# The value matmuls of two attention pairs as one group in one PSUM bank, with the input that is made last read first

## The chip, the cores and the metric

The kernel runs on one core of one Trainium2 chip. The metric is the device time of an execution in microseconds (us); the time of a kernel is the median of its runs. Times inside an execution come from the trace of one profiled execution.

## The reference

One block of a streaming encoder, for 256 tokens of width 2048: a normalisation, one wide projection, then two branches side by side (an HGRN2 recurrence with 8 heads, and attention in chunks of 64 tokens with 16 heads), merged by gates, an output projection, and an MLP of width 8192. The change lies in the attention branch, between the projections of q, k and v (each 1024 wide) and the projection `w_branch_b`:

```
def chunk_band_attention(q, k, v, rel_bias):     # (B, H, T, Dh): H = 16, T = 256, Dh = 64
    # each chunk of 64 queries sees its own chunk and the 8 before it (all of the past, at T = 256)
    ...
    s = jnp.einsum('bhnqd,bhnkd->bhnqk', qc, kb).astype(jnp.float32) * (Dh ** -0.5) + bias[:, None]
    s = jnp.where(valid[:, None, :], s, -jnp.inf)
    p = jax.nn.softmax(s, axis=-1).astype(v.dtype)
    o = jnp.einsum('bhnqk,bhnkd->bhnqd', p, vb)
```

## The kernel before, in words

**The large projections.** Weights come from HBM in pieces `raw_...` by DMAs that SP issues. ACT casts each to fp32r (`wh_...`, L91) and DVE subtracts the cast from the original (`wl_...`, L92); this is `split`. PE then forms a product from a high and a low part: for q and k in `mm_t` (accumulators `acc_aq`, `acc_ak`; L178 with 512 columns for the high part, L183 with 256 for the low one), for the rest in `mm3` (L136 to L138, 512 columns each; `acc_av...` are the values v, `acc_ga0...` the first gate projection). These matmuls fill nearly all of PE's stream. `aq2` and `ak2` are the third quarter of q and k, and so on.

**Attention.** Sixteen heads go two at a time, as a pair; the pairs 0 to 3 are called 00 to 03, the pairs 4 to 7 10 to 13 (the first digit is the half of `yb` into which they go). `attn_pair` computes the scores of a pair (L595, eight short matmuls into PSUM tile `s00` ... `s13`) and calls `attn_head` twice. A head has 256 queries in two blocks of 128: the first sees 128 keys, the second 256, so its scores are 128 x 384. For each head:

- POOL fetches the bias (L601) and fills the corner with a large negative number (L602).
- DVE adds the bias (L604, L605) and takes the maxima (L607, L608).
- ACT takes exp with sums (L610, L611): 128 columns, then 256.
- DVE inverts the sums and scales the two blocks (L614, 128 columns, then L615, 256) in the SBUF tile `sb`, of which there are two.
- PE transposes the three blocks of 128 columns (L618) into a PSUM tile `tpp`; ACT copies it to SBUF (`pt`, L620; four buffers).

**The values.** `attn_values` multiplies the transposed probabilities of a pair with v, in a PSUM tile `pa`: four matmuls with 64 output rows each (L631). Two have 256 columns and take the keys 0 to 127 (`av00`, or `av10` for the second half), two have 128 columns and take the keys 128 to 255 (`av01`, `av11`); of each two the second head of the pair goes first. `split` then writes the result as high part (ACT cast) and low part (DVE subtraction) into `act_yb`, the left operand of the projection `w_branch_b`, which comes after the gate projections.

**What sets the order.** The tile framework schedules all instructions when the kernel is built, by priorities and its own estimates of time, so the order of each engine's queue is fixed, and every engine works its queue in that order. The scores and the values have a raised priority (`high_priority`). In the source, the values of a pair are called one pair later than its heads, and so stand behind the next pair's. `tpp` and `pa` share the two buffers of one PSUM pool (`ps_tp`, tag "tp"), so a new one of either kind needs the one before last to be read out.

Of the kernel before, what the change touches and what calls it, by code (L numbers as in the profile page):

```python
# [8 lines left out]
F32 = mybir.dt.float32  # L9
# [7 lines left out]
P = 128  # L17
T = 256
# [32 lines left out]
def tile_hybrid_block(  # L51
# [5 lines left out]
    nc = tc.nc  # L57
# [158 lines left out]
    for kt, n in zip(starts, steps):  # L216
        c, a = kt // 4, kt % 4
# [380 lines left out]
    def attn_head(hd, ps):  # L598
        bias = bp.tile([P, T], F32, name=f"bias{hd}", tag="bias", bufs=3)
        rb = rel_bias[hd]  # L600
        nc.gpsimd.dma_start(bias, bass.AP(tensor=rb.tensor, offset=rb.offset + P + 1, ap=[[1, P], [1, T]]))  # L601
        nc.gpsimd.memset(bias[0:CH, 0:CH], NEG)  # L602
        s = bp.tile([P, 3 * P], F32, name=f"sb{hd}", tag="s", bufs=2)
        nc.vector.tensor_tensor(s[:, 0:P], ps[:, 0:P], rev(bias[:, 0:P]), op=ALU.add)  # L604
        nc.vector.tensor_tensor(s[:, P:], ps[:, P:], rev(bias), op=ALU.add)  # L605
        mx = small.tile([P, 2], F32, name=f"mx{hd}", tag="mx")
        nc.vector.tensor_reduce(mx[:, 0:1], s[:, 0:P], axis=AX.X, op=ALU.max, negate=True)  # L607
        nc.vector.tensor_reduce(mx[:, 1:2], s[:, P:], axis=AX.X, op=ALU.max, negate=True)  # L608
        sums = small.tile([P, 2], F32, name=f"sum{hd}", tag="sums")
        nc.scalar.activation(s[:, 0:P], s[:, 0:P], AF.Exp, bias=mx[:, 0:1], accum_out=sums[:, 0:1])  # L610
        nc.scalar.activation(s[:, P:], s[:, P:], AF.Exp, bias=mx[:, 1:2], accum_out=sums[:, 1:2])  # L611
        rs = small.tile([P, 2], F32, name=f"rs{hd}", tag="rs")
        nc.vector.reciprocal(rs, sums)
        nc.vector.tensor_scalar(s[:, 0:P], s[:, 0:P], rs[:, 0:1], None, op0=ALU.mult)  # L614
        nc.vector.tensor_scalar(s[:, P:], s[:, P:], rs[:, 1:2], None, op0=ALU.mult)  # L615
        tp = ps_tp.tile([P, 3, P], F32, name=f"tpp{hd}", tag="tp")
        for i in range(3):
            nc.tensor.transpose(tp[:, i, :], s[:, i * P:(i + 1) * P], ident)  # L618
        pt = bp.tile([P, 3, P], F32, name=f"pt{hd}", tag="pt", bufs=4)
        nc.scalar.copy(pt, tp)  # L620
        return pt

    def attn_values(g, pr, pts, vs):

        hi, lo = yb[g][:, :, 0, :], yb[g][:, :, 1, :]
        po = ps_tp.tile([P, T], F32, name=f"pa{g}{pr}", tag="tp")
        with tc.high_priority(offset=2000):
            for i, src, dst in ((0, slice(0, 2), slice(0, T)), (1, slice(2, 3), slice(P, T))):
                for j, pt in ((1, pts[1]), (0, pts[0])):
                    r = slice(64 * j, 64 * j + 64)  # L630
                    nc.tensor.matmul(po[r, dst], vs[i][:, P * pr + 64 * j:P * pr + 64 * j + 64], pt[:, src, :].rearrange("p a t -> p (a t)"),  # L631
                                     start=i == 0, stop=i == 1, skip_group_check=True)
        split(hi[:, pr, :], lo[:, pr, :], po)

    def token(what, pool=None):
        if pool is not None:
# [77 lines left out]
    pairs = {}  # L714
# [229 lines left out]

    qT = [qk_chunk(C_AQ + i * T, f"aq{i}", rstd8_t, acc_q[i]) for i in range(2)]
    kT = [qk_chunk(C_AK + i * T, f"ak{i}", rstd_t) for i in range(2)]
    pts = None
    for i in range(4):
        if i > 1:
            qT.append(qk_chunk(C_AQ + i * T, f"aq{i}", rstd8_t))  # L950
# [2 lines left out]
            alone(Unit(lambda: xT, lambda: Sx, w_in_n, C_AV, "av", values))  # L953
        if not i % 2:
            yb.append(new_act(f"yb{i // 2}"))
        for pr in (2 * i, 2 * i + 1):
            last, pts = pts, attn_pair(pr // 4, pr % 4, qT[i][:, pr % 2, :], kT[i][:, pr % 2, :])
            if last:
                attn_values((pr - 1) // 4, (pr - 1) % 4, last, av[(pr - 1) // 4])
    attn_values(1, 3, pts, av[1])  # L960

    ga, gb = [], []
    units = []
# [247 lines left out]
```

## Time and profile before

| what | value |
|---|---|
| time, median of 3 runs | 1389.49 us (1389.38 to 1389.76) |
| profiled execution, own time | 1389.94 us |
| its span in the trace | 1388.1 us (1.84 us lie around it) |
| attention heads on PE, first transpose to last value group | 266.9 to 391.0 us |
| value matmuls (`pa`) | 64 records, first 304.9 us, last 390.7 us |
| casts of `pa` on ACT (L91) | 8, median 372 ns |
| subtractions of `pa` on DVE (L92) | 8, median 418 ns |
| transposes (`tpp`) | 48, median 273 ns |
| copies to `pt` on ACT (L620) | 16, median 479 ns |

How to read it: PE is busy nearly all the time, and the length that is shown for a matmul overlaps with the next one's (matmuls are pipelined). What a matmul costs PE's stream is therefore read from start to start, not from its length. A value matmul of the program leaves two records. The attention heads are spread thinly between the matmuls of the projections; in the trace's rows, `x8` counts the records that one row takes together.

### The profile page before, as it was taken

What the parts mean: (1) busy time and instruction counts of PE and PEld (TensorE: products, weight loads), DVE (VectorE), ACT (ScalarE), POOL (GpSimd) and SP (SyncE); (2) the same over time, 40 slices, a digit from 0 to 9 for tenths busy, and PEclk for the clock granted to TensorE, in tenths of its full rate; (3) what the DMA queues carried; (4) which work ended last, traced back from release to release, by engine and by line L of the source; (5) the groups of instructions that cost most, each with busy time, mean ns of one, the idle gap of its engine ahead of it and who ended that gap; (6) DMA issues with size and microseconds to landing.
All of it is one profiled execution on the core that took longest, in us unless ns stands there. A gap on an engine that the chain in (4) does not pass through costs nothing.

```text
span 1388.1 us, 18593 instructions
## 1 busy us (share of the span) xinstructions
PE 1376.7 (99%) x6550; PEld 1143.5 (82%) x6550; DVE 1137.7 (82%) x1417; ACT 922.7 (66%) x1185; POOL 143.4 (10%) x227
## 2 busy tenths in 40 slices
PE   9999999999999999999999999999999999999997
PEld 8889888878778888888888888888888888888886
DVE  7897988876878775698998977879877888878886
ACT  6765645665676664346777766678666876668864
POOL 3000001101100000001211011200011001110200
PEclk9999999999999999999999999999999999999999
DMA  9654446685669886558979789988899889998892
GB/s 328 235 178 141 163 166 239 169 284 169 175 199 284 261 266 226 189 168 273 301 215 310 245 259 300 261 255 244 251 298 295 248 223 263 276 297 265 255 276 105
DMA packets 124077, 331.61 MB, mean 239 GB/s; under 512 B 11072, under 2 KB 11840, under 8 KB 123600
## 3 DMA queue, kind: packets, MB, share of 16 engines
q1 hardware_dynamic: 103696, 265.59, 54.4%
q0 software_dynamic: 19568, 64.04, 23.5%
q8 instruction: 51, 0.84, 0.2%
q10 hardware_dynamic: 720, 0.81, 0.2%
q14 instruction: 42, 0.34, 0.1%
HBM read 271.67 MB, written 10.49 MB: 203 GB/s over the span
## 4 chain that ended last, share of the span: by engine, by line
PE 89%; DMA 5%; DVE 3%; issue 2%; ACT 1%; POOL 0%; POOLq 0%; SPq 0%; ACTq 0%; DVEq 0%
PE acc_ak L178 2%; PE acc_aq L178 2%; PE acc_hf L178 2%; PE acc_hq L178 2%; PE ps L415 1%; PE acc_ak L183 1%; PE acc_hg L137 1%; PE acc_hi L137 1%; PE acc_bb L136 1%; PE acc_hi L138 1%; PE acc_hg L136 1%; PE acc_bb L137 1%; PE acc_ba L136 1%; PE acc_hi L136 1%; PE acc_ba L138 1%
## 5 line engine op out<-in xcount | busy, mean ns | idle before, releaser
L178 PE MATMUL acc_aq<-act_x,wh_aq 128*128 128x512 f32 x128 | 41.7, 402 | 0.0
L178 PE MATMUL acc_hf<-act_x,wh_hf 128*128 128x512 f32 x128 | 40.8, 400 | 0.1
L178 PE MATMUL acc_hq<-act_x,wh_hq 128*128 128x512 f32 x128 | 40.7, 400 | 0.0
L178 PE MATMUL acc_ak<-act_x,wh_ak 128*128 128x512 f32 x128 | 40.4, 397 | 0.0
L91 ACT CAST wh_bb<-raw_bb 128x1024 fp32r<-128x1024 f32 x16 | 16.9, 1054 | 23.3 <-PE acc_ba L138 17.7
L92 DVE TENSOR_TENSOR wl_bb<-raw_bb,wh_bb 128x1024 fp32r<-128x1024 f32 x16 | 19.6, 1223 | 14.8 <-ACT wh_bb L91 14.8
L91 ACT CAST wh_ba<-raw_ba 128x1024 fp32r<-128x1024 f32 x16 | 16.8, 1052 | 19.9 <-PE acc_bb L138 13.8
L92 DVE TENSOR_TENSOR wl_aq<-raw_aq,wh_aq 128x1024 fp32r<-128x1024 f32 x16 | 19.5, 1222 | 12.5 <-ACT wh_aq L91 12.5
L92 DVE TENSOR_TENSOR wl_ba<-raw_ba,wh_ba 128x1024 fp32r<-128x1024 f32 x16 | 19.5, 1223 | 11.6 <-ACT wh_ba L91 11.6
L183 PEld LDWEIGHTS acc_hq<-act_x,wl_hq 128*128 128x128 f32 x128 | 23.4, 188 | 6.6 <-DVE wl_hq L92 1.4
L91 ACT CAST wh_aq<-raw_aq 128x1024 fp32r<-128x1024 f32 x16 | 16.7, 1051 | 17.1 <-PE acc_hg L138 7.3
L183 PEld LDWEIGHTS acc_hf<-act_x,wl_hf 128*128 128x128 f32 x128 | 23.4, 188 | 5.5 <-DVE wl_hf L92 0.3
L183 PEld LDWEIGHTS acc_ak<-act_x,wl_ak 128*128 128x128 f32 x128 | 23.5, 188 | 5.3
L183 PEld LDWEIGHTS acc_aq<-act_x,wl_aq 128*128 128x128 f32 x128 | 23.3, 188 | 5.1 <-issue 0.3
L92 DVE TENSOR_TENSOR act_u<-tp_u,act_u 128x512 fp32r<-128x512 f32 x32 | 21.9, 685 | 4.7 <-ACT act_u L91 4.2
L183 PE MATMUL acc_hq<-act_x,wl_hq 128*128 128x256 f32 x128 | 24.7, 280 | 1.0 <-DVE wl_hq L92 1.0
L136 PE MATMUL acc_hg<-wh_hg,act_x 128*128 128x512 f32 x64 | 25.6, 400 | 0.0
L183 PE MATMUL acc_aq<-act_x,wl_aq 128*128 128x256 f32 x128 | 25.6, 284 | 0.0
L136 PE MATMUL acc_hi<-wh_hi,act_x 128*128 128x512 f32 x64 | 25.5, 399 | 0.0
L92 DVE TENSOR_TENSOR wl_hf<-raw_hf,wh_hf 128x1024 fp32r<-128x1024 f32 (+2 forms) x21 | 20.5, 976 | 6.1 <-ACT wh_hf L91 5.7
L91 ACT CAST wh_ak<-raw_ak 128x1024 fp32r<-128x1024 f32 x16 | 16.8, 1051 | 12.9 <-PE acc_aq L178 5.5
L136 PE MATMUL acc_bb<-wh_bb,act_yb 128*128 128x512 f32 x64 | 25.2, 393 | 0.0
(1928 smaller groups left out, 5237.3 us busy)
## 6 DMA issues: line engine op xcount, KB each, us to landing
raw_hi<-in_w_in_n_dram SPq DMA_DIRECT2D x16, 512.0 KB, 4.5
raw_hg<-in_w_in_n_dram SPq DMA_DIRECT2D x16, 512.0 KB, 3.5
raw_aq<-in_w_in_t_dram SPq DMA_DIRECT2D x16, 512.0 KB, 3.7
raw_ak<-in_w_in_t_dram SPq DMA_DIRECT2D x16, 512.0 KB, 4.8
raw_ba<-in_w_branch_a_dram SPq DMA_DIRECT2D x16, 512.0 KB, 4.6
raw_bb<-in_w_branch_b_dram SPq DMA_DIRECT2D x16, 512.0 KB, 4.7
raw_hf<-in_w_in_t_dram SPq DMA_DIRECT2D x12, 512.0 KB, 3.6
raw_hq<-in_w_in_t_dram SPq DMA_DIRECT2D x12, 512.0 KB, 4.0
```

The costliest lines, as they stand in the source:

```text
L91: casts[:] = [(copy or nc.scalar.copy)(hi, src)]
L92: return nc.vector.tensor_tensor(lo, src, hi.bitcast(F32), op=ALU.subtract)
L136: nc.tensor.matmul(acc, hi, wh, start=first, stop=False, skip_group_check=True)
L137: nc.tensor.matmul(acc, hi, wl, start=False, stop=False, skip_group_check=True)
L138: nc.tensor.matmul(acc, lo, wh, start=False, stop=last, skip_group_check=True)
L178: nc.tensor.matmul(acc[:, cb, :], wh[:, cb * P:(cb + 1) * P], r.rearrange("p u t -> p (u t)"), start=kt == 0, stop=last)
L183: nc.tensor.matmul(acc[:, cb, 0:T], wl[:, cb * P:(cb + 1) * P], r[:, 0, :], start=False, stop=False)
L415: nc.tensor.matmul(ps[:, m, :], klf[:, a * P:(a + 1) * P], qrf[:, a * 192:(a + 1) * 192], start=True, stop=True)
```

## The change

Three edits in the attention branch:

1. The three transposes of a head are issued in the order 1, 2, 0, so the first one reads the block that is scaled last (L615), and the one that was first reads the block scaled by L614.
2. `attn_values` takes two pairs at a time. Its PSUM tile holds both (2 x 256 columns of 4 bytes, a whole bank), and its eight matmuls begin with the second pair, so with the head whose probabilities are made last. The evictions become one cast and one subtraction of 2 x 256 columns for two pairs.
3. The values of two pairs are called directly behind the two pairs' heads, no longer one pair later.

The program has four value groups then, `pa00`, `pa02`, `pa10` and `pa12`, of eight matmuls each (before: `pa00` to `pa03` and `pa10` to `pa13`, of four), and four casts of ACT and four subtractions of DVE fewer. PE has 6380 matmuls before and after. The order of SP is the same; on POOL only the DMA of bias 10 and the memset of bias 9 change places.

```diff
--- before.py
+++ after.py
@@ -614,23 +614,24 @@
         nc.vector.tensor_scalar(s[:, 0:P], s[:, 0:P], rs[:, 0:1], None, op0=ALU.mult)
         nc.vector.tensor_scalar(s[:, P:], s[:, P:], rs[:, 1:2], None, op0=ALU.mult)
         tp = ps_tp.tile([P, 3, P], F32, name=f"tpp{hd}", tag="tp")
-        for i in range(3):
+        for i in (1, 2, 0):
             nc.tensor.transpose(tp[:, i, :], s[:, i * P:(i + 1) * P], ident)
         pt = bp.tile([P, 3, P], F32, name=f"pt{hd}", tag="pt", bufs=4)
         nc.scalar.copy(pt, tp)
         return pt
 
-    def attn_values(g, pr, pts, vs):
+    def attn_values(g, p0, pairs, vs):
 
         hi, lo = yb[g][:, :, 0, :], yb[g][:, :, 1, :]
-        po = ps_tp.tile([P, T], F32, name=f"pa{g}{pr}", tag="tp")
+        po = ps_tp.tile([P, 2, T], F32, name=f"pa{g}{p0}", tag="tp")
         with tc.high_priority(offset=2000):
-            for i, src, dst in ((0, slice(0, 2), slice(0, T)), (1, slice(2, 3), slice(P, T))):
-                for j, pt in ((1, pts[1]), (0, pts[0])):
-                    r = slice(64 * j, 64 * j + 64)
-                    nc.tensor.matmul(po[r, dst], vs[i][:, P * pr + 64 * j:P * pr + 64 * j + 64], pt[:, src, :].rearrange("p a t -> p (a t)"),
-                                     start=i == 0, stop=i == 1, skip_group_check=True)
-        split(hi[:, pr, :], lo[:, pr, :], po)
+            for p, pts in ((1, pairs[1]), (0, pairs[0])):
+                for i, src, dst in ((0, slice(0, 2), slice(0, T)), (1, slice(2, 3), slice(P, T))):
+                    for j, pt in ((1, pts[1]), (0, pts[0])):
+                        r, c = slice(64 * j, 64 * j + 64), P * (p0 + p) + 64 * j
+                        nc.tensor.matmul(po[r, p, dst], vs[i][:, c:c + 64], pt[:, src, :].rearrange("p a t -> p (a t)"),
+                                         start=i == 0, stop=i == 1, skip_group_check=True)
+        split(hi[:, p0:p0 + 2, :], lo[:, p0:p0 + 2, :], po)
 
     def token(what, pool=None):
         if pool is not None:
@@ -944,7 +945,6 @@
 
     qT = [qk_chunk(C_AQ + i * T, f"aq{i}", rstd8_t, acc_q[i]) for i in range(2)]
     kT = [qk_chunk(C_AK + i * T, f"ak{i}", rstd_t) for i in range(2)]
-    pts = None
     for i in range(4):
         if i > 1:
             qT.append(qk_chunk(C_AQ + i * T, f"aq{i}", rstd8_t))
@@ -953,11 +953,9 @@
             alone(Unit(lambda: xT, lambda: Sx, w_in_n, C_AV, "av", values))
         if not i % 2:
             yb.append(new_act(f"yb{i // 2}"))
-        for pr in (2 * i, 2 * i + 1):
-            last, pts = pts, attn_pair(pr // 4, pr % 4, qT[i][:, pr % 2, :], kT[i][:, pr % 2, :])
-            if last:
-                attn_values((pr - 1) // 4, (pr - 1) % 4, last, av[(pr - 1) // 4])
-    attn_values(1, 3, pts, av[1])
+        g, p0 = i // 2, i % 2 * 2
+        both = [attn_pair(g, p0 + p, qT[i][:, p, :], kT[i][:, p, :]) for p in range(2)]
+        attn_values(g, p0, both, av[g])
 
     ga, gb = [], []
     units = []
```

In the queues' rows the number behind a name tells the buffer. PE, from the transposes of head 3 on, before (behind them: the projection `aq2`, the transposes of heads 4 and 5, the scores `s03`):

```order
L618 MATMUL tpp3_3045<-ident_78,sb3_3032 128x128
L631 MATMUL pa00_3051<-pt1_3000,av00_2912 64x256
L631 MATMUL pa00_3051<-pt0_2978,av00_2912 64x256
L631 MATMUL pa00_3051<-pt1_3000,av01_2914 64x128
L631 MATMUL pa00_3051<-pt0_2978,av01_2914 64x128
L618 MATMUL tpp3_3045<-ident_78,sb3_3032 128x128 x2
L178 MATMUL acc_aq2_3171<-act_x0_107,wh_aq2_0_3173 128x512 x2
L183 MATMUL acc_aq2_3171<-act_x0_107,wl_aq2_0_3174 128x256 x2
L178 MATMUL acc_aq2_3171<-act_x0_107,wh_aq2_0_3173 128x512 x2
L183 MATMUL acc_aq2_3171<-act_x0_107,wl_aq2_0_3174 128x256 x2
L178 MATMUL acc_aq2_3171<-act_x0_107,wh_aq2_0_3173 128x512
L618 MATMUL tpp4_3079<-ident_78,sb4_3066 128x128 x3
```

The same place in the changed kernel:

```order
L618 MATMUL tpp3_3045<-ident_78,sb3_3032 128x128 x3
L178 MATMUL acc_aq2_3172<-act_x0_107,wh_aq2_0_3174 128x512 x2
L183 MATMUL acc_aq2_3172<-act_x0_107,wl_aq2_0_3175 128x256 x2
L178 MATMUL acc_aq2_3172<-act_x0_107,wh_aq2_0_3174 128x512
L595 MATMUL s03_3111<-ak1T_2533,aq1T_2436 128x128 x2
L595 MATMUL s03_3111<-ak1T_2533,aq1T_2436 128x256 x2
L178 MATMUL acc_aq2_3172<-act_x0_107,wh_aq2_0_3174 128x512
L632 MATMUL pa00_3051<-pt3_3049,av00_2912 64x256
L632 MATMUL pa00_3051<-pt2_3027,av00_2912 64x256
L632 MATMUL pa00_3051<-pt3_3049,av01_2914 64x128
L632 MATMUL pa00_3051<-pt2_3027,av01_2914 64x128
L632 MATMUL pa00_3051<-pt1_3000,av00_2912 64x256
L632 MATMUL pa00_3051<-pt0_2978,av00_2912 64x256
```

The group `pa00` stood between the transposes of head 3 and read the probabilities of heads 0 and 1. Now it stands behind the scores `s03` and begins with `pt3`, the copy of those transposes; the transposes of heads 3 and 4 are each in one piece.

PE around the transposes of head 14 (`ga0` is the first gate projection), before:

```order
L137 MATMUL acc_ga0c11_3796<-wl_ga0p21A2_3921,S2_x_2426 128x512
L138 MATMUL acc_ga0c11_3796<-wh_ga0p21A2_3920,S2_x_2426 128x512
L136 MATMUL acc_ga0c11_3796<-wh_ga0p21A2_3920,S2_x_2426 128x512
L618 MATMUL tpp14_3732<-ident_78,sb14_3719 128x128
L137 MATMUL acc_ga0c11_3796<-wl_ga0p21A2_3921,S2_x_2426 128x512
L618 MATMUL tpp14_3732<-ident_78,sb14_3719 128x128 x2
L138 MATMUL acc_ga0c11_3796<-wh_ga0p21A2_3920,S2_x_2426 128x512
L136 MATMUL acc_ga0c22_3824<-wh_ga0r1_10_3936,act_x2_109 128x512
L137 MATMUL acc_ga0c22_3824<-wl_ga0r1_10_3937,act_x2_109 128x512
```

And in the changed kernel:

```order
L136 MATMUL acc_ga0c11_3784<-wh_ga0p21A2_3908,S2_x_2426 128x512
L137 MATMUL acc_ga0c11_3784<-wl_ga0p21A2_3909,S2_x_2426 128x512
L138 MATMUL acc_ga0c11_3784<-wh_ga0p21A2_3908,S2_x_2426 128x512
L136 MATMUL acc_ga0c22_3812<-wh_ga0r1_10_3924,act_x2_109 128x512
L137 MATMUL acc_ga0c22_3812<-wl_ga0r1_10_3925,act_x2_109 128x512
L138 MATMUL acc_ga0c22_3812<-wh_ga0r1_10_3924,act_x2_109 128x512
L618 MATMUL tpp14_3723<-ident_78,sb14_3710 128x128 x3
L136 MATMUL acc_ga0c22_3812<-wh_ga0r1_10_3924,act_x2_109 128x512
L137 MATMUL acc_ga0c22_3812<-wl_ga0r1_10_3925,act_x2_109 128x512
L138 MATMUL acc_ga0c22_3812<-wh_ga0r1_10_3924,act_x2_109 128x512
```

The transposes of head 14 were split by L137; now they stand in one piece, and five matmuls of the gate projection that stood behind their first stand ahead of it.

ACT behind the evictions of v (`av11`), before:

```order
L938 ACTIVATE av11_2950<-acc_avc22_2676,rstd_522 128x512
L620 COPY pt3_3049<-tpp3_3045 128x384
L91 CAST act_yb0_2952<-pa00_3051 128x256
L620 COPY pt4_3083<-tpp4_3079 128x384
L610 ACTIVATE sb5_3088,sum5_3094<-sb5_3088,mx5_3091 128x128
L611 ACTIVATE sb5_3088,sum5_3094<-sb5_3088,mx5_3091 128x256
L91 CAST wh_ak2_0_3266<-raw_ak2_0_3265 128x1024
L91 CAST act_yb0_2952<-pa01_3107 128x256
L620 COPY pt5_3105<-tpp5_3101 128x384
L610 ACTIVATE sb6_3122,sum6_3128<-sb6_3122,mx6_3125 128x128
```

And in the changed kernel:

```order
L939 ACTIVATE av11_2950<-acc_avc22_2676,rstd_522 128x512
L620 COPY pt3_3049<-tpp3_3045 128x384
L610 ACTIVATE sb5_3092,sum5_3098<-sb5_3092,mx5_3095 128x128
L611 ACTIVATE sb5_3092,sum5_3098<-sb5_3092,mx5_3095 128x256
L91 CAST act_yb0_2952<-pa00_3051 128x2x256
L620 COPY pt4_3087<-tpp4_3083 128x384
L620 COPY pt5_3109<-tpp5_3105 128x384
L610 ACTIVATE sb6_3119,sum6_3125<-sb6_3119,mx6_3122 128x128
L91 CAST wh_ak2_0_3267<-raw_ak2_0_3266 128x1024
L611 ACTIVATE sb6_3119,sum6_3125<-sb6_3119,mx6_3122 128x256
```

The queue is the same up to the copy `pt3`. Then the cast of `pa00` is twice as wide and stands behind the exp of head 5; the cast of `pa01` is gone, and the weights' cast `wh_ak2_0` stands further back, behind `pt5`.

## The prediction

> **What bounds the kernel now.** I read the busy shares first, then the chain that ended last, and last the timeline of the stretch that the change touches.
>
> ```profile
> PE 1376.7 (99%) x6550; PEld 1143.5 (82%) x6550; DVE 1137.7 (82%) x1417; ACT 922.7 (66%) x1185; POOL 143.4 (10%) x227
> PE 89%; DMA 5%; DVE 3%; issue 2%; ACT 1%; POOL 0%; POOLq 0%; SPq 0%; ACTq 0%; DVEq 0%
> ```
>
> PE is busy 99%, and it is 89% of the chain. The window of the attention heads, as start and length, then the busy time of PE, weight loads, DVE, ACT and POOL with their instructions, the granted clock, and DMA:
>
> ```profile
> 304.40:391.30 86.90, 86.13 (x499) 66.80 (x499) 67.81 (x129) 54.31 (x105) 8.98 (x20) 1.00 0.64 189
> ```
>
> Between 304.4 us (where the first value group stands) and 391.3 us (behind the last), PE idles 0.8 us at a granted clock of 1.00; DVE idles 19 us and ACT 33 us. So PE is bound by its own stream, one instruction starting behind another, and I price everything by start-to-start times on PE. What PE loses or wins there is passed on whole, since after it PE is again the engine that sets the pace. All instructions ahead of 304.4 us and behind 391.3 us keep their order on every engine.
>
> **The unit prices.** A lone value group (pa13 of before, the last), in the timeline of PE (start, length, instruction, count of records):
>
> ```profile
> 389.81 0.40 PE L138 MATMUL acc_ga0c<-wh_ga0p21B,S_x 128*128 128x512 f32 x1
> 390.14 0.87 PE L631 MATMUL pa<-pt,av 128*64 128x256 f32 x8
> 390.94 0.50 PE L136 MATMUL acc_ga0c<-wh_ga0r,act_x 128*128 128x512 f32 x1
> 391.27 0.39 PE L137 MATMUL acc_ga0c<-wl_ga0r,act_x 128*128 128x512 f32 x1
> ```
>
> From 389.81 to 391.27 are 1.46 us, of which two ordinary matmuls take 0.227 each (their step everywhere in this stage); the group costs **1.01**. Of it 0.80 lies between its first start and the next matmul's; the other **0.21** is paid at the edges: 0.33 instead of 0.23 ahead of it, 0.33 instead of 0.23 behind it.
>
> A group between the transposes of another head, as seven of the eight stand:
>
> ```profile
> 378.37 0.39 PE L136 MATMUL acc_ga0c<-wh_ga0p21A,S_x 128*128 128x512 f32 x1
> ...
> 379.88 0.48 PE L137 MATMUL acc_ga0c<-wl_ga0p21A,S_x 128*128 128x512 f32 x1
> 380.19 0.39 PE L138 MATMUL acc_ga0c<-wh_ga0p21A,S_x 128*128 128x512 f32 x1
> ```
>
> 1.82 less 0.45 is 1.37 for three transposes and a group. Three transposes in one piece:
>
> ```profile
> 307.13 0.40 PE L183 MATMUL acc_aq<-act_x,wl_aq 128*128 128x256 f32 x2
> 307.36 0.40 PE L178 MATMUL acc_aq<-act_x,wh_aq 128*128 128x512 f32 x1
> 307.59 0.49 PE L618 MATMUL tpp<-ident,sb 128*128 128x128 f32 x3
> 307.84 0.48 PE L178 MATMUL acc_aq<-act_x,wh_aq 128*128 128x512 f32 x1
> ```
>
> They take 0.25, and the matmul behind them starts its successor 0.09 late (0.31 for 0.23 from 379.88 to 380.19): **0.34**. So 1.37 is 1.03 + 0.34: a group costs the same between transposes as alone. A projection matmul steps by 0.23 (L178, 307.36 to 307.59), a pair of half length by 0.23 (L183, 307.13 to 307.36).
>
> **Term 1, four merges: -0.84.** Eight groups become four of twice the length; each loses one pair of edges, 4 x 0.21. The trace has no group of eight value matmuls, so the saving is bounded: if the edges belong to each change of operands inside, nothing is saved (0); if only the columns counted (eight records of 1536 columns, two at a time, at 512 per 0.227 us: 0.34), each merge would save 1.01 - 0.34 = 0.67, together -2.7. I take the row nearest to it, the lone group's.
>
> From 390.94 to 391.27 the trace shows 0.10 of the edge behind the group. The Trainium skill (TensorE: Matmul & The Clock Gate, "Step-by-step: what each phase is for") has weight loads pulled ahead of matmuls in flight; by that this 0.10 would be hidden, the merges would give -0.44, and the time would be 1388.7; the row shows it unhidden. The Trainium skill (TensorEngine Tiling (Array Packing), Key Properties) says that changing the tiling mode drains TensorE; value groups use half-width tiles, so by it the edges belong to the whole group, and the sum stays as above; the trace's 0.33 ahead and behind agrees.
>
> **Term 2, transposes in one piece: -0.15.** Five sets (heads 6, 10, 12, 14, 15) are split by ordinary matmuls or a group. Head 6:
>
> ```profile
> 314.35 0.30 PE L618 MATMUL tpp<-ident,sb 128*128 128x128 f32 x1
> 314.41 0.36 PE L183 MATMUL acc_aq<-act_x,wl_aq 128*128 128x256 f32 x1
> 314.61 0.38 PE L618 MATMUL tpp<-ident,sb 128*128 128x128 f32 x2
> 314.75 0.36 PE L183 MATMUL acc_aq<-act_x,wl_aq 128*128 128x256 f32 x1
> 314.95 0.63 PE L178 MATMUL acc_aq<-act_x,wh_aq 128*128 128x512 f32 x2
> ```
>
> 0.60 less two L183 (0.23) is 0.37 against 0.34 whole; five times 0.03.
>
> **Term 3, PE's waits for the probabilities: -0.61.** Four sets start late in before. Head 5:
>
> ```profile
> 309.45 0.63 PE L178 MATMUL acc_aq<-act_x,wh_aq 128*128 128x512 f32 x2
> 310.25 0.30 PE L618 MATMUL tpp<-ident,sb 128*128 128x128 f32 x1 [0.17 <-DVE sb L614]
> ```
>
> Head 9:
>
> ```profile
> 341.91 0.63 PE L178 MATMUL acc_aq<-act_x,wh_aq 128*128 128x512 f32 x2
> 342.70 0.33 PE L618 MATMUL tpp<-ident,sb 128*128 128x128 f32 x1 [0.16 <-DVE sb L614]
> ```
>
> Head 12, and head 14:
>
> ```profile
> 375.32 0.40 PE L137 MATMUL acc_ga0c<-wl_ga0r,act_x 128*128 128x512 f32 x1
> 375.68 0.33 PE L618 MATMUL tpp<-ident,sb 128*128 128x128 f32 x1
> ```
>
> ```profile
> 381.81 0.39 PE L136 MATMUL acc_ga0c<-wh_ga0p21A,S_x 128*128 128x512 f32 x1
> 382.25 0.30 PE L618 MATMUL tpp<-ident,sb 128*128 128x128 f32 x1
> ```
>
> Less the matmuls' own steps they wait 0.34 (head 5), 0.33 (head 9), 0.13 (head 12) and 0.21 (head 14). The new order starts a set with the block scaled last, by L615 behind L614:
>
> ```profile
> 309.83 0.28 DVE L614 TENSOR_SCALAR sb<-sb,rs 128x128 f32<-128x128 f32 x1
> 310.02 0.35 DVE L615 TENSOR_SCALAR sb<-sb,rs 128x256 f32<-128x256 f32 x1
> ```
>
> so a set can begin 0.19 + 0.07 = 0.26 later than before. Head 12 now has two more matmuls ahead of it (0.45) and head 14 five (1.1): both waits go, -0.34. Head 5 comes behind the first merged group and its input is no longer late: -0.34. Head 9 has only one more L183 (0.12) ahead: 0.26 - 0.12, +0.14 at most, of which I count +0.07, since pa03 no longer covers the later block. Bounds: all of them gone, -1.0; none gone and each 0.26 longer, +1.0.
>
> **Term 4, the first merged group waits for pt3: +0.25.** The new wait stands at the head of PE's queue, and every projection matmul behind it waits too. ACT reaches the copy of pt3 as before, since its queue is the same up to there:
>
> ```profile
> 304.88 1.05 ACT L91 CAST wh_aq<-raw_aq 128x1024 fp32r<-128x1024 f32 x1 [1.67 <-PE acc_avc L138]
> 305.83 1.26 ACT L938 ACTIVATE av<-acc_avc,rstd 128x512 f32<-128x512 f32 x2
> 306.99 0.48 ACT L620 COPY pt<-tpp 128x384 f32<-128x384 f32 x1
> ```
>
> The copy is ready at 307.47. How soon PE uses one is seen at pa13, which began at 390.14:
>
> ```profile
> 389.55 0.48 ACT L620 COPY pt<-tpp 128x384 f32<-128x384 f32 x1 [0.73 <-PE tpp L618]
> ```
>
> 0.11 behind the copy; so pa00 can start at 307.58. PE's own arrival follows from head 3's transposes, whose start does not move, and the price of a group of scores:
>
> ```profile
> 304.68 0.27 PE L618 MATMUL tpp<-ident,sb 128*128 128x128 f32 x1
> ```
>
> ```profile
> 363.69 0.93 PE L595 MATMUL s<-ak3T,aq3T 64*128 64x128 f32 x8
> 364.55 0.50 PE L137 MATMUL acc_ga0c<-wl_ga0p11A,act_x 128*128 128x512 f32 x1
> ```
>
> 304.68 + 0.34 + three L178 and two L183 (0.92) + scores (0.86 and edges of 0.21: 1.07) + one L178 and an edge (0.33) = 307.34. PE waits 0.24, taken as 0.25. Bounds: none, and one more cast of ACT in front (0.95, its step from 304.88 to 305.83).
>
> **Term 5, the other three merged groups: +0.15.** In before head 15's last two transposes start at 389.13:
>
> ```profile
> 389.13 0.38 PE L618 MATMUL tpp<-ident,sb 128*128 128x128 f32 x2
> ```
>
> and the group that reads their copy at 390.14, 1.01 us later. In the new order that place holds two L178 and two single L183 after head 7, three L178 after head 11 and five ga0 matmuls after head 15; with the transposes' own 0.25 and the edge of 0.10 that is 1.0, 1.0 and 1.5 us: just enough, or 0.05 to 0.1 short twice. Bounds: 0, and 0.95 each when a cast of ACT stands in front.
>
> **At nothing:** the wider evictions (four casts and four subtractions for eight each) take less time of ACT and DVE together, and both idle in the window; without that cover one would cost a cast's 0.95. The outputs are first read by acc_bb, a whole gate stage later.
>
> **Sum:** -0.84 - 0.15 - 0.61 + 0.25 + 0.15 = **-1.20 us**. The profiled execution took 1389.94 us (span 1388.1 and 1.84 around it), so 1388.74 there. It lies 0.45 above the median of the runs, 1389.49: **1388.3 us** as a median.
>
> **Rivals.**
> *A, merging saves nothing at the edges.* Then -0.36: 1389.1 us. For it: no longer group is in the trace. Against it: the edges stand outside the group's 0.80.
> *B, slower: the merged groups wait for ACT.* Before, a pair's values ran one pair later, when their copies were long made; now each group waits for the newest copy, in order, with only 1.0 us of cover against 1.01 needed. Its place is heads 7, 11 and 15. If a cast (0.95) stands ahead of the copy each time, +2.85 in place of 0.15: +1.5, **1391.0 us**. It decides from 1.6 us of such waits on. For it: ACT's new queue has wh_ak2_4 ahead of pt6 and pt7, and wh_ga0p21D0 ahead of pt15. Against it: these casts run while PE still does other matmuls. The Trainium skill (the same TensorE page and section) says that matmuls themselves stay in program order, which is this rival's premise.
> *C, more is saved:* edges worth twice as much (-1.7), the four waits gone (-1.0), term 2 as it is, terms 4 and 5 nothing: -2.85, 1386.6 us. For it: the bound of term 1. Against it: each wait removed lets PE reach the next input sooner.
> That the change does not do what it says is excluded by the order: groups of eight and whole sets stand there, except head 1's, which stays split.
>
> **Chances.** Forecast 0.60 (1387.6 to 1389.0), A 0.16, B 0.13, C 0.07, something unseen 0.04. The range 1387.0 to 1390.6 leaves out most of C (0.05), two thirds of B (0.09) and the unseen. About 0.2%, 2.8 us, is what a measurement of this kernel can tell from no change: below 1386.7 lie 0.05 of C and 0.01 unseen, above 1392.3 0.04 of B and 0.02 unseen.
>
> **What would show it.** Term 1: a merged group's 16 records in about 1.6 us from first start to the next matmul, edges 0.33. Term 2: no lone transpose beside an ordinary matmul behind 304 us. Term 3: no late start at heads 5, 12 and 14. Term 4: pa at 307.6 with a wait on ACT pt. B shows as PE gaps released by ACT pt or weight loads held for it ahead of the other three groups; I am wrong if these sum to over 1.6 us, or if DVE or ACT makes a weight half late behind them.

## The result, and the profile after

| | before | changed |
|---|---|---|
| median of 22 runs each | 1389.32 us (1388.40 to 1390.94) | 1387.90 us (1386.95 to 1389.00) |
| profiled execution, own time | 1389.94 us | 1388.95 us |
| span | 1388.1 us | 1387.1 us |
| stretch of the heads on PE | 105.68 us | 104.05 us |

The ratio of changed to before is 0.9988, with a 95% interval of 0.9983 to 0.9994: 0.8 to 2.4 us faster. Forecast were 1388.3 us and a gain of 1.20. Most of the chance (0.88) lay on a change of less than 0.2%, and 0.12% is less.

The two lines of the page that answer to those of before:

```profile
PE 1375.5 (99%) x6550; PEld 1144.4 (83%) x6550; DVE 1137.2 (82%) x1413; ACT 922.2 (66%) x1181; POOL 143.3 (10%) x227
PE 96%; DMA 1%; ACT 1%; DVE 1%; issue 0%; SPq 0%; POOLq 0%; POOL 0%; ACTq 0%; DVEq 0%
```

PE is still the bound; why the chain's share of PE rose from 89% to 96% was not followed up. Whole executions differ by more than the change is worth: the span is 1.0 us shorter, but PE reaches the heads 0.99 us later than before, in a part of the program that is the same. So from here on I measure the **stretch**: from the start of the last matmul of `acc_avc` (ahead of the transposes of head 3) to the start of the first matmul of `acc_ga2c`, both of which stand in the same place in all kernels. In the windows view (start:end and length, then PE, weight loads, DVE, ACT and POOL with instructions, clock, DMA), before:

```profile
304.45:410.13 105.68, 104.91 (x582) 82.35 (x580) 80.69 (x141) 65.81 (x117) 9.84 (x21) 1.00 0.65 191
```

And of the changed kernel:

```profile
305.44:409.49 104.05, 103.26 (x582) 82.78 (x581) 80.28 (x137) 65.02 (x113) 9.79 (x21) 1.00 0.66 195
```

1.63 us less, with as many matmul records (582) and PE's idle time unchanged (0.77 and 0.79): the gain is time in which PE is shown busy. In a second profiled execution of the changed kernel the stretch was 104.01, 0.04 us less.

The last value group, in PE's timeline, to be held against the lone group of before:

```profile
388.52 0.39 PE L138 MATMUL acc_ga0c<-wh_ga0p21B,S_x 128*128 128x512 f32 x1
388.84 1.52 PE L632 MATMUL pa<-pt,av 128*64 128x256 f32 x16
390.29 0.50 PE L136 MATMUL acc_ga0c<-wh_ga0r,act_x 128*128 128x512 f32 x1
390.63 0.40 PE L137 MATMUL acc_ga0c<-wl_ga0r,act_x 128*128 128x512 f32 x1
```

From 388.52 to 390.63 are 2.11 us; less two steps of 0.227 the group of eight costs **1.66**, where two groups of four cost 2.02. A merge saves 0.36 (0.366 before rounding), not the 0.21 of the prediction, and four of them 1.46.

Where the other 0.15 came from could be read in the trace of before. Windows that begin inside its last group (pa13, first start 390.14, next matmul 390.94) show the starts of its pairs of records:

```profile
390.40 0.60 PE L631 MATMUL pa<-pt,av 128*64 128x256 f32 x6
390.62 0.39 PE L631 MATMUL pa<-pt,av 128*64 128x128 f32 x4
390.73 0.28 PE L631 MATMUL pa<-pt,av 128*64 128x128 f32 x2
```

Each row here covers what is left of the group, so its start is that of the next pair. The steps are 0.26, 0.22, 0.11 and 0.21. The two records of a pair start together (7 ns apart); 256 columns take 0.22 and 128 columns 0.11. So the first step is 0.05 too long and the last 0.10: parts of the edges that lie inside the 0.80 which I had taken as the group's own. Edges in all: 0.10 + 0.05 + 0.10 + 0.10 = 0.35, and 0.65 for the work.

The weight loads (PEld) of before change at the same two places:

```profile
390.14 0.63 PEld L631 LDWEIGHTS pa<-pt,av 128*64 128x64 f32 x8 [0.37 <-ACT pt L620]
390.94 0.19 PEld L136 LDWEIGHTS acc_ga0c<-wh_ga0r,act_x 128*128 128x128 f32 x1 [0.17 <-ACT u_ga L759]
```

The group's first load starts with its matmul (390.14), and so does that of the matmul behind the group (390.94), while the L138 ahead has its load 0.23 before it (389.58 and 389.81). So at both edges no load ran ahead. The waits on ACT that these two rows name are not needed for it: in e9 below, a group whose copies were long made starts with its load too (366.54). That the late loads are the whole of the edges was not tested.

### The profile page after: what moved, and what is told of

It reads as the page before. It is cut to its first block, busy times and chain, and to the rows that moved or that the text cites. A ratio compares the mean times of both kernels' runs of the same rounds, so it can differ in the third digit from the quotient of the medians.

```text
span 1387.1 us, 18586 instructions
## 1 busy us (share of the span) xinstructions
PE 1375.5 (99%) x6550; PEld 1144.4 (83%) x6550; DVE 1137.2 (82%) x1413; ACT 922.2 (66%) x1181; POOL 143.3 (10%) x227
## 4 chain that ended last, share of the span: by engine, by line
PE 96%; DMA 1%; ACT 1%; DVE 1%; issue 0%; SPq 0%; POOLq 0%; POOL 0%; ACTq 0%; DVEq 0%
PE acc_ak L178 2%; PE acc_hf L178 2%; PE acc_hq L178 2%; PE acc_aq L178 2%; PE ps L415 1%; PE acc_hq L183 1%; PE acc_ak L183 1%; PE tp_u L109 1%; PE acc_hf L183 1%; PE acc_hi L137 1%; PE acc_hg L137 1%; PE acc_bb L136 1%; PE acc_ba L138 1%; PE acc_hg L136 1%; PE acc_hi L138 1%; PE acc_hg L138 1%
## 5 line engine op out<-in xcount | busy, mean ns | idle before, releaser
L178 PE MATMUL acc_aq<-act_x,wh_aq 128*128 128x512 f32 x128 | 41.7, 402 | 0.0
L178 PE MATMUL acc_hf<-act_x,wh_hf 128*128 128x512 f32 x128 | 41.1, 403 | 0.0
L178 PE MATMUL acc_hq<-act_x,wh_hq 128*128 128x512 f32 x128 | 40.8, 400 | 0.0
L178 PE MATMUL acc_ak<-act_x,wh_ak 128*128 128x512 f32 x128 | 40.4, 397 | 0.0
L183 PEld LDWEIGHTS acc_hf<-act_x,wl_hf 128*128 128x128 f32 x128 | 23.4, 188 | 6.5 <-DVE wl_hf L92 1.4
L183 PEld LDWEIGHTS acc_hq<-act_x,wl_hq 128*128 128x128 f32 x128 | 23.4, 188 | 6.2 <-DVE wl_hq L92 1.0
L183 PEld LDWEIGHTS acc_ak<-act_x,wl_ak 128*128 128x128 f32 x128 | 23.4, 188 | 5.4 <-issue 0.2
L183 PEld LDWEIGHTS acc_aq<-act_x,wl_aq 128*128 128x128 f32 x128 | 23.4, 188 | 5.0 <-issue 0.2
L183 PE MATMUL acc_aq<-act_x,wl_aq 128*128 128x256 f32 x128 | 25.8, 283 | 0.0
L183 PE MATMUL acc_hf<-act_x,wl_hf 128*128 128x256 f32 x128 | 24.7, 280 | 0.7 <-DVE wl_hf L92 0.7
L183 PE MATMUL acc_hq<-act_x,wl_hq 128*128 128x256 f32 x128 | 24.7, 279 | 0.6 <-DVE wl_hq L92 0.6
L137 PE MATMUL acc_hi<-wl_hi,act_x 128*128 128x512 f32 x64 | 24.9, 390 | 0.0
```

The costliest lines, as they stand in the source:

```text
L137: nc.tensor.matmul(acc, hi, wl, start=False, stop=False, skip_group_check=True)
L178: nc.tensor.matmul(acc[:, cb, :], wh[:, cb * P:(cb + 1) * P], r.rearrange("p u t -> p (u t)"), start=kt == 0, stop=last)
L183: nc.tensor.matmul(acc[:, cb, 0:T], wl[:, cb * P:(cb + 1) * P], r[:, 0, :], start=False, stop=False)
```

## The experiments

The first theory, **adjacency**: the gain is the edges of the groups that no longer exist, 0.36 each, wherever eight value matmuls stand in a row. Its rivals: **order** (the gain comes from transposes that are neither split nor late) and **one bank** (from one PSUM tile and half the evictions). "Stretch" is that defined above; times are medians, beside those of the kernel before on the same chip. Their ratios have intervals of 0.09% on either side (1.25 us), e6's 0.12%, so what differs by less than that is told apart by the stretch alone. The stretch is held against one trace of before, and differences of some 0.1 us in it lie near what two executions differ by.

| kernel | stretch, us | against before | time, us | before, us |
|---|---|---|---|---|
| changed | 104.05 | -1.63 | 1387.90 | 1389.32 |
| e1 transposes' order alone | 106.53 | +0.85 | 1390.28 | 1389.65 |
| e3 first pair first | 105.64 | -0.04 | 1389.96 | 1389.65 |
| e5 two banks | 104.08 | -1.60 | 1387.45 | 1389.65 |
| e6 group twice | 109.26 | +3.58 | 1393.17 | 1389.65 |
| e2 old order of the transposes | 104.48 | -1.20 | 1388.45 | 1389.03 |
| e8 last group out of the gap | 104.96 | -0.72 | 1388.85 | 1389.03 |
| e9 third group into a gap | 103.98 | -1.70 | 1387.68 | 1389.03 |
| e7 three buffers of sb | 105.38 | -0.30 | 1389.61 | 1389.03 |
| e10 e1 with its last group in the gap | 105.57 | -0.11 | 1389.12 | 1388.96 |
| changed, again | 104.01 | -1.67 | 1387.98 | 1388.96 |
| e9, again | 104.00 | -1.68 | 1387.43 | 1388.96 |

**e6, the price inside a group.**

```diff
-            for p, pts in ((1, pairs[1]), (0, pairs[0])):
+            for p, pts in ((1, pairs[1]), (0, pairs[0])) * 2:
```

> The changed kernel with each group's eight matmuls issued twice in a row, 16 matmuls in one group, with the same result. It measures the price inside a group without its edges. Theory 'adjacency': eight more matmuls inside a group cost two times 0.65 us (the step of four within the merged group), so 4 x 1.30 = 5.2 us more than the changed kernel, 1393.1. If edges were paid at every change of operands inside: 4 x 1.65 = 6.6 more, 1394.5. If only the columns counted at the pace of the projections (512 in 0.227 us, two halves at a time): 4 x 0.68 = 2.7 more, 1390.6.

The stretch is 5.21 us longer than the changed kernel's, and the time 1393.17. The last group in its timeline:

```profile
395.37 0.39 PE L138 MATMUL acc_ga0c<-wh_ga0p21B,S_x 128*128 128x512 f32 x1
395.69 2.82 PE L632 MATMUL pa<-pt,av 128*64 128x256 f32 x32
398.44 0.50 PE L136 MATMUL acc_ga0c<-wh_ga0r,act_x 128*128 128x512 f32 x1
398.77 0.40 PE L137 MATMUL acc_ga0c<-wl_ga0r,act_x 128*128 128x512 f32 x1
```

3.40 less 0.454 is 2.95 for 16 matmuls, 1.29 more than for eight: 0.65 for four, without edges. So a group of four is 0.65 + 0.36, one of eight 1.30 + 0.36. Both other prices of the expectation are out.

**e5, two PSUM tiles.** The eight matmuls keep their order, the tiles and evictions are those of before:

```diff
-        po = ps_tp.tile([P, 2, T], F32, name=f"pa{g}{p0}", tag="tp")
+        po = [ps_tp.tile([P, T], F32, name=f"pa{g}{p0 + p}", tag="tp") for p in range(2)]
...
-        split(hi[:, p0:p0 + 2, :], lo[:, p0:p0 + 2, :], po)
+        for p in range(2):
+            split(hi[:, p0 + p, :], lo[:, p0 + p, :], po[p])
```

> The changed kernel with the eight matmuls in the same order one behind another, but into two PSUM tiles of one pair each, with two casts and two subtractions as before the change. Theory 'adjacency': the edges go all the same, 1387.7 to 1388.3 us if the changed kernel is 1387.9; it needs both buffers of the pool at once, which may hold the next transposes by up to 0.5 us. Rival 'one bank': the saving is lost, 1389.0 to 1389.4.

```profile
305.32:409.40 104.08, 103.32 (x582) 82.69 (x580) 80.85 (x141) 65.47 (x117) 9.98 (x21) 1.00 0.65 195
```

DVE and ACT have four instructions more each (141 and 117), PE's stretch is the changed kernel's to 0.03 us. So the one bank and the fewer evictions are worth nothing that is seen; the gain comes with the row of eight. The rival "one bank" falls.

**e3, the first pair's matmuls first.**

```diff
-            for p, pts in ((1, pairs[1]), (0, pairs[0])):
+            for p, pts in ((0, pairs[0]), (1, pairs[1])):
```

> The changed kernel with the first pair's matmuls ahead of the second pair's. One PSUM tile, one cast and one subtraction for two pairs, as in the change; but the scheduler now puts the first four matmuls of pa00, pa10 and pa12 further ahead, so that only pa02 is eight matmuls in a row: seven groups on PE. Theory 'adjacency': only one of four mergers saves its 0.36 us, so the stretch comes out about 1.1 us longer than in the changed kernel, less the wait of pa00 (0.29): 0.7 to 1.1 us longer; 1388.6 to 1389.0 us if the changed kernel is 1387.9. Rival 'one bank' (one PSUM tile and half the evictions are what saves): as fast as the changed kernel, within 0.2 us, 1387.7 to 1388.1.

The time was 1389.96, and the stretch 1.59 longer than the changed kernel's: more than adjacency allowed for, and I had no term for the rest. The order of the matmuls is no ornament: with the old inputs first, the scheduler issues the first half of three groups as soon as it can, and the group that is one in the source is two in the queue.

**e1, the transposes' order alone.** The kernel before with

```diff
-        for i in range(3):
+        for i in (1, 2, 0):
             nc.tensor.transpose(tp[:, i, :], s[:, i * P:(i + 1) * P], ident)
```

> The kernel before with only the transposes' order 1, 2, 0. Its PE queue keeps eight value groups of four matmuls; the sets of heads 6, 10, 12 and 14 come in one piece. Theory 'adjacency' (what is saved is the pair of edges of each group that disappears, 0.36 us each, 1.46 of the 1.63 us that the trace of the changed kernel gained between the last acc_avc matmul and the first matmuls behind the last value group): no group disappears, so only the whole sets (4 x 0.03) and the waits of heads 12 and 14 (0.34) go: 0.2 to 0.6 us less in that stretch, 1388.7 to 1389.1 us if before is 1389.3. Rival 'order' (the gain comes from transposes that no longer wait and are no longer split): 1.2 to 1.6 us less, 1387.7 to 1388.1.

A miss for both theories: 0.85 us *longer*, 1390.28 us. The place, in PE's timeline:

```profile
390.42 0.40 PE L138 MATMUL acc_ga0c<-wh_ga0p21B,S_x 128*128 128x512 f32 x1
391.49 0.50 PE L136 MATMUL acc_ga0c<-wh_ga0r,act_x 128*128 128x512 f32 x1 [0.68 <-ACT u_ga L759]
```

1.07 us between two matmuls that are 0.23 apart elsewhere, 0.84 too many. Behind the last L138 of ga0p21B the accumulator is copied by ACT before ga0r can add to it. In the kernel before pa13 stands in this wait, in the changed one pa12; in e1 and e3 the last value matmuls stand two ordinary ones earlier, and the wait lies open. Hence a second theory, **gap**: that place gives any group 0.85 us for nothing. Three kernels test it.

**e8, the last group out of the gap.** The call of the last group is held back and pinned behind the 12 matmuls of the first ga0r piece (`last_mm` holds the last L138 issued; `issue_after` sets the queue's order and adds no wait):

```diff
-        attn_values(g, p0, both, av[g])
+        if i != 3:
+            attn_values(g, p0, both, av[g])
+        else:
+            held_back.append(lambda g=g, p0=p0, both=both: attn_values(g, p0, both, av[g]))
...
         u.plain(0, (8, 9))
+        if held_back:
+            with tc.issue_after(last_mm[0].ins):
+                held_back.pop()()
```

> The changed kernel with the last merged group (pa12) 12 matmuls of ga0r further back, all else in place. Theory 'gap': behind the last L138 of ga0p21B PE has to wait for ACT's copy u_ga, and pa12 lies in that wait; when it is moved away, the 0.85 us that e1 and e3 show there come out, and the group still costs its 1.65: the stretch gets 0.85 us longer than in the changed kernel, 1388.7 to 1388.8 us if that is 1387.9. Rival 'no gap' (what e1 and e3 lost there came from their ACT or DVE queues, which differ too): within 0.2 us of the changed kernel.

```profile
388.04 0.40 PE L138 MATMUL acc_ga0c<-wh_ga0p21B,S_x 128*128 128x512 f32 x1
389.11 0.50 PE L136 MATMUL acc_ga0c<-wh_ga0r,act_x 128*128 128x512 f32 x1 [0.68 <-ACT u_ga L760]
389.45 0.40 PE L137 MATMUL acc_ga0c<-wl_ga0r,act_x 128*128 128x512 f32 x1
```

In ACT's timeline of the same kernel, the copy that ends the wait:

```profile
388.47 0.58 ACT L760 COPY u_ga<-acc_ga0c 128x512 f32<-128x512 f32 x1 [0.25 <-PE acc_ga0c L138]
```

ACT begins the copy 0.43 behind the start of the last matmul and ends it at 389.05; PE goes on at 389.11. The stretch is 0.91 longer than the changed kernel's, 0.85 expected. The gap is shown, and it is a little wider than the theory had it: the matmul behind the wait is followed 0.34 later instead of 0.23 (389.11 to 389.45), which makes 0.84 + 0.11 = 0.95 us that a group standing there covers.

**e10, e1 with its last group in the gap.** As e1, and

```diff
-    attn_values(1, 3, pts, av[1])
+    held_back.append(lambda: attn_values(1, 3, pts, av[1]))
...
         u.product("21", "B", u.comb(7))
+        if held_back:
+            with tc.issue_after(last_mm[0].ins):
+                held_back.pop()()
```

> The kernel before with the transposes' order 1, 2, 0 (as e1), and with the last value group (pa13) put back behind the last L138 of ga0p21B, where PE waits for u_ga. In e1 the group stood two matmuls ahead of that place, and the stretch was 0.85 us longer than before. Theory 'gap': it is 0.85 us shorter than in e1, so equal to before within 0.15 us, 1389.0 to 1389.4 us if before is 1389.2; the order of the transposes alone is worth nothing in the kernel before. Rival: the loss of e1 stays, or only part of it goes.

```profile
305.48:411.05 105.57, 104.69 (x581) 82.84 (x580) 80.97 (x141) 65.79 (x117) 9.87 (x21) 1.00 0.65 191
```

0.96 shorter than e1 and 0.11 shorter than before. So e1's loss was the gap, and the transposes' order alone is worth 0.1 us at most. With it the larger part of e3 is understood: 0.95 of gap, and three groups split again (3 x 0.36 = 1.08) less the wait of pa00, which is gone there (0.18, see term 4 below). That is 1.85 against the 1.59 measured; the other 0.26 was not followed up.

**e2, the change with the old order of the transposes.**

```diff
-        for i in (1, 2, 0):
+        for i in range(3):
```

> The changed kernel with the transposes of a head in the old order 0, 1, 2; four merged value groups, the last of them in its place behind the last L138 of ga0p21B. The stretch is that of PE from the last acc_avc matmul to the matmuls behind the last value group; it was 1.63 us shorter in the changed kernel than before. Theory 'adjacency': nearly all of it stays, since the merged groups stay and the order of the transposes alone gained nothing in e1 beside the gap: five sets split again (5 x 0.03 us) and 0 to 0.4 us of waits, so the stretch is 1.1 to 1.6 us shorter than before; 1387.9 to 1388.4 us if the changed kernel is 1387.9. Rival 'order': without it at most 0.6 us of the gain is left, 1388.9 or more.

```profile
304.40:408.88 104.48, 103.78 (x581) 82.47 (x580) 80.33 (x137) 65.03 (x113) 9.93 (x21) 1.00 0.65 192
```

1.20 us shorter than before, inside what adjacency allowed: three quarters of the gain stay without the new order; the order adds 0.43 to the merge, though alone it gave 0.11, so the two do not simply add up. The rival "order" falls as the main cause.

**e9, the third group into another gap.** The traces so far have a second gap. In the changed kernel:

```profile
368.92 0.39 PE L138 MATMUL acc_ga0c<-wh_ga0p22A,S_x 128*128 128x512 f32 x1
369.14 0.50 PE L136 MATMUL acc_ga0c<-wh_ga0p11D,act_x 128*128 128x512 f32 x1
369.97 0.50 PE L136 MATMUL acc_ga0c<-wh_ga0p12C,S_x 128*128 128x512 f32 x1 [0.33 <-ACT acc_ga0c L760]
370.30 0.39 PE L137 MATMUL acc_ga0c<-wl_ga0p12C,S_x 128*128 128x512 f32 x1
```

From 368.92 to 370.30 three steps take 1.38 us instead of 0.68, so this gap is worth 0.70.

e9 holds pa10 back (and, since `pt` has four buffers, the heads behind it) until the copy that PE waits for is issued (L760, in `u.begun`):

```diff
-        both = [attn_pair(g, p0 + p, qT[i][:, p, :], kT[i][:, p, :]) for p in range(2)]
-        attn_values(g, p0, both, av[g])
+        heads = lambda g=g, p0=p0, i=i: [attn_pair(g, p0 + p, qT[i][:, p, :], kT[i][:, p, :]) for p in range(2)]
+        if i < 2:
+            attn_values(g, p0, heads(), av[g])
+        elif i < 3:
+            held_back.append(lambda both=heads(): attn_values(1, 0, both, av[1]))
+        else:
+            held_back.append(lambda: attn_values(1, 2, heads(), av[1]))
...
         u.begun("12", "22")
+        if held_back:
+            with tc.issue_after(last_mm[0].ins):
+                held_back.pop(0)()
+            held_back.pop()()
```

> The changed kernel with the third merged group (pa10) moved from 350 us, where it covers nothing, into the other wait that every trace shows, behind the last L138 of ga0p22A, where the first matmul of ga0p12C waits for ACT's copy of an accumulator (0.60 us more than a step, with one matmul in between). Theory 'gap': the group still costs 1.65 us, but 0.6 to 0.7 us of it fall where PE waits anyway: the stretch is 0.6 to 0.7 us shorter than in the changed kernel, 1387.2 to 1387.3 us if that is 1387.9, faster than both. Rival 'no gap': no change, or longer, if the wait moves on with the group.

```profile
366.22 0.39 PE L138 MATMUL acc_ga0c<-wh_ga0p22A,S_x 128*128 128x512 f32 x1
366.54 1.52 PE L632 MATMUL pa<-pt,av 128*64 128x256 f32 x16
367.99 0.50 PE L136 MATMUL acc_ga0c<-wh_ga0p12C,S_x 128*128 128x512 f32 x1
```

The group went into the gap, and yet the stretch is only 0.07 shorter: a miss. What was won came back as waits. Head 14's set in e9:

```profile
381.41 0.39 PE L137 MATMUL acc_ga0c<-wl_ga0r,act_x 128*128 128x512 f32 x1
381.76 0.52 PE L618 MATMUL tpp<-ident,sb 128*128 128x128 f32 x3
382.04 0.47 PE L138 MATMUL acc_ga0c<-wh_ga0r,act_x 128*128 128x512 f32 x1
382.35 0.39 PE L136 MATMUL acc_ga0c<-wh_ga0r,act_x 128*128 128x512 f32 x1
```

and in the changed kernel:

```profile
383.03 0.40 PE L138 MATMUL acc_ga0c<-wh_ga0r,act_x 128*128 128x512 f32 x1
383.26 0.49 PE L618 MATMUL tpp<-ident,sb 128*128 128x128 f32 x3
383.50 0.47 PE L136 MATMUL acc_ga0c<-wh_ga0r,act_x 128*128 128x512 f32 x1
383.82 0.39 PE L137 MATMUL acc_ga0c<-wl_ga0r,act_x 128*128 128x512 f32 x1
```

0.94 against 0.79, less the same steps: 0.48 against 0.34. DVE's scaling ahead of it, in e9 and then in the changed kernel:

```profile
381.27 0.34 DVE L615 TENSOR_SCALAR sb<-sb,rs 128x256 f32<-128x256 f32 x1
```

```profile
382.68 0.35 DVE L615 TENSOR_SCALAR sb<-sb,rs 128x256 f32<-128x256 f32 x1
```

In e9 L615 ends at 381.61; PE's turn had come at 381.64 (a step behind 381.41), but the set starts at 381.76. In the changed kernel L615 ends at 383.03 and the set starts at 383.26, just when its turn comes. So PE, now earlier, waits for DVE; worked out in the same way the four sets of heads 12 to 15 cost 0.23, 0.15, 0.14 and 0.16 more, 0.68 together, nearly the 0.70 of the gap. What holds DVE there, and whether it could be earlier, was not tried.

> The kernel of e9 beside the changed kernel. In e9's trace the group fell into the gap, but the transposes of heads 12 to 15 then each cost 0.14 to 0.23 us more, since they reach their scaled scores earlier; the stretch was 0.07 us shorter at its end than the changed kernel's, and 0.5 us shorter 75 us further on. If that later gain is the kernel's own: 0.4 to 0.6 us faster than the changed kernel. If it was one execution's chance: within 0.2 us of it.

Beside the changed kernel on the same chip e9 took 1387.43 us against 1387.98. Each has its own interval against before (0.9980 to 0.9998, and 0.9983 to 1.0001), and the stretches are equal (104.00 and 104.01), so e9 is not shown to be faster. The changed kernel itself:

> The changed kernel itself, on the same chip as the next. By the result, 1.2 to 1.6 us less than before.

It came out 0.98 us below before, less than forecast, with an interval that holds the 1.4 and also no gain at all.

**e7, a third buffer for sb.**

```diff
-        bias = bp.tile([P, T], F32, name=f"bias{hd}", tag="bias", bufs=3)
+        bias = bp.tile([P, T], F32, name=f"bias{hd}", tag="bias", bufs=2)
...
-        s = bp.tile([P, 3 * P], F32, name=f"sb{hd}", tag="s", bufs=2)
+        s = bp.tile([P, 3 * P], F32, name=f"sb{hd}", tag="s", bufs=3)
```

> The changed kernel with three buffers for the scaled scores sb in place of two, and two for the bias in place of three, so that it fits. In its queue pa00 and the transposes of heads 4 to 7 stand elsewhere. Of the waits that are left on PE, that of pa00 for pt3 (0.29 us) and that of head 9 for L615 (0.52 us) could go. If these waits come from the buffer of sb: 0.3 to 0.8 us shorter than the changed kernel, 1387.1 to 1387.6 us if that is 1387.9. If they come from the chain of DVE itself: within 0.2 us. If two bias buffers are too few: longer, by waits of DVE's L604 for the bias.

The scores s03 stand ahead of the stretch here, so their 1.06 is added: 105.38, 1.33 longer than the changed kernel's. DVE's timeline, and behind it PE's, in e7:

```profile
380.95 0.29 DVE L604 TENSOR_TENSOR sb<-s,bias 128x128 f32<-128x128 f32 x1 [1.33 <-POOL bias L602]
```

```profile
383.56 0.52 PE L618 MATMUL tpp<-ident,sb 128*128 128x128 f32 x3 [1.21 <-ACT wh_ga0r L91]
```

Two bias buffers are too few: head 15's first add waits 1.33 us for the bias, and head 14's scaling, queued behind it on DVE, comes late. (PE's row names a cast of ACT that ends at 383.56; the transposes read what L615 scales, which ends at 383.42, 0.14 ahead of them, about as in e9.) Less the 1.4 us that head 14's set costs too much, the stretch would be 104.0, the changed kernel's. In this order of the queue pa00 does not wait, but head 9 waits 0.26 longer for L615 than in the changed kernel. So no gain of the third buffer is seen; as two sizes and the order were changed, it settles no more than that.

## Why the prediction was right, point by point

The time (1388.3 forecast, 1387.9 measured), the sign and the range held, and the case forecast is the one that happened, with one of its terms mis-sized. The time alone cannot tell a gain of 1.20 from one of 1.63, both of which lie in its interval; the stretch can, and there the forecast is 0.43 short. Term by term:

| term | forecast | trace of the changed kernel |
|---|---|---|
| 1, four merges | -0.84 | -1.46 |
| 2, sets in one piece | -0.15 | -0.15 |
| 3, waits for the scaled scores | -0.61 | -0.49, and +0.18 at head 11 |
| 4, pa00 waits for pt3 | +0.25 | +0.18 |
| 5, the other merged groups wait | +0.15 | 0 |
| sum | -1.20 | -1.74 (stretch: -1.63) |

The terms come to 0.11 more than the stretch; about as much is what the ordinary steps, outside all groups, sets and waits, differ by between the two traces. That the errors of terms 3, 4 and 5 cancel to 0.08 was luck.

**Term 1 was mis-sized.** The step that failed is "of it 0.80 lies between its first start and the next matmul's; the other 0.21 is paid at the edges": 0.15 of the 0.80 is edge as well (e6: 0.65 for four matmuls, so 0.36 of 1.01). The bound "if only the columns counted" was not reached either: value columns, two records at a time, take 0.85 ns each, as 256 in 0.22, not the 0.44 ns of the projections' 512 in 0.227. That the edges belong to the group, and not to changes of operands inside, is shown by e6; that a bank has no part in it, by e5. What makes the edge is less clear: the value matmuls are half as wide as their neighbours, but the transposes, which have the full width, show 0.09 behind them too (380.41 to 380.73 in the changed kernel, 0.32 for 0.23) and nothing ahead. Rival A is excluded: it held that a merge saves nothing.

**Term 2 held.** The sets stand whole, at 0.34 each, as with head 14 above.

**Term 3 was right at heads 5, 12 and 14, where no late start is left (-0.68), and wrong in size at head 9.** There the set begins with the block scaled last, and the matmul that was added ahead of it covers less than I counted:

```profile
343.59 0.28 PE L183 MATMUL acc_aq<-act_x,wl_aq 128*128 128x256 f32 x1
344.18 0.55 PE L618 MATMUL tpp<-ident,sb 128*128 128x128 f32 x3 [0.31 <-DVE sb L615]
344.48 0.36 PE L183 MATMUL acc_aq<-act_x,wl_aq 128*128 128x256 f32 x1
344.68 0.63 PE L178 MATMUL acc_aq<-act_x,wh_aq 128*128 128x512 f32 x2
```

From 343.59 to 344.68 are 1.09 us; less two halves of L183 (0.23) and the whole set (0.34) it waits 0.52, where it had waited 0.33: +0.19, against +0.07. Head 11 had no wait before and has one now:

```profile
348.82 0.39 PE L178 MATMUL acc_aq<-act_x,wh_aq 128*128 128x512 f32 x1
349.21 0.52 PE L618 MATMUL tpp<-ident,sb 128*128 128x128 f32 x3
349.48 0.48 PE L178 MATMUL acc_aq<-act_x,wh_aq 128*128 128x512 f32 x1
349.80 0.39 PE L178 MATMUL acc_ak<-act_x,wh_ak 128*128 128x512 f32 x1
```

0.98 less 0.46 and 0.34 is 0.18. My sum looked only at heads that were late before; a set that starts with its latest input can also become late where it was not. Nor did the sum find all that were late: head 7 starts 0.21 late in before (0.44 behind the L178 at 317.05), and it is late by 0.2 in the changed kernel too (316.25), so nothing changed there.

**Term 4 happened, at 0.18.** The copy of pt3, in ACT's timeline, and PE's wait for it:

```profile
307.98 0.48 ACT L620 COPY pt<-tpp 128x384 f32<-128x384 f32 x1
```

```profile
307.89 0.50 PE L178 MATMUL acc_aq<-act_x,wh_aq 128*128 128x512 f32 x1
308.51 1.52 PE L632 MATMUL pa<-pt,av 128*64 128x256 f32 x16
```

The copy ends at 308.46, pa00 starts 0.05 later, and 0.62 behind L178. This L178 stands right behind the scores `s03`, and the edge behind a group of scores lies in its step even where nothing follows, as behind the next scores:

```profile
337.72 0.50 PE L178 MATMUL acc_aq<-act_x,wh_aq 128*128 128x512 f32 x1
338.06 0.40 PE L183 MATMUL acc_aq<-act_x,wl_aq 128*128 128x256 f32 x2
```

With that 0.34 and the 0.10 ahead of a value group, 0.44 of the 0.62 is no wait, and 0.18 is. The prediction's own sum, which counts the edges of the scores, gives the same: 305.67, where the transposes of head 3 start, + 0.34 + 0.92 + 1.07 + 0.33 is 308.33, 0.18 ahead of 308.51. The expectations of e3 and e7 had 0.29, without the edge of the scores. The 0.11 that the prediction took from pa13 was no time of waiting either: pa13 starts 0.33 behind its neighbour, a step and an edge, so just in its turn.

**Term 5** did not occur: pa12 above starts 0.32 behind the matmul ahead of it, a step and an edge, and the trace shows the same of pa10 (350.35, 0.33) and of pa02 (317.40, 0.20 behind a matmul of half length, whose step is 0.12). So rival B, which needed 1.6 us of such waits, did not happen. C did not happen as a whole, but its term for the edges (-1.7) came nearer to the -1.46 than the forecast's -0.84.

What the forecast did not see is the gap. It counted pa13 as 1.01 us of PE's time when PE would have lost 0.95 of that anyway; that this did no harm to the sum is luck, since the changed kernel happens to put its own last group in the same place. Out of it, the change gives back more than half of its gain (e8: 0.91 of 1.63).

## What to carry to other kernels

A short group of matmuls of another shape can pay a fixed price for going in and out: 0.36 us here, for groups of 4, 8 and 16 alike. Read it from a group's own inner steps, not from the distance between its neighbours, and save it by putting such groups side by side on PE, in one bank or two. Here the scheduler kept them side by side when their first matmul needed the latest input, and split three of four when it needed the older one (e3). Before an edit moves work, look for the waits that this work covers: a row that reads like pure cost may stand in a wait that opens when it goes.

## What was not expected of the hardware

- Going into a value group (128 x 64, f32) from ordinary matmuls and out of it costs 0.10 + 0.05 and 0.10 + 0.10 us; inside, the records start in pairs 7 ns apart, and a pair of 256 columns takes 0.22 us, one of 128 columns 0.11. The loads of weights at both edges start with their matmuls (390.14 and 390.94 in before), not ahead of them.
- PE takes up a copy of ACT 0.05 to 0.06 us after it ends (pa00 at 308.51 behind 308.46; e8, 389.11 behind 389.05), and a scaling of DVE 0.15 us after (e9, 381.76 behind 381.61).
- An accumulator that ACT has to copy before PE goes on costs PE 0.84 us (388.04 to 389.11 in e8, less a step) and 0.11 more at the matmul behind it (389.11 to 389.45).
